# A decoder layer's token mixer: one offset step moved, one pair of VectorE steps swapped, one output tile stored in halves

## The chip, the cores and the metric

The kernel runs on one core of one Trainium2 chip. The core has five engines with queues of their own: TensorE (matrix products), VectorE and ScalarE (elementwise work, and the only ones here that read what TensorE leaves in PSUM), GpSimd, and SyncE, which here issues most of the DMA transfers. The metric is the device time of one execution in microseconds, as the median of several executions.

## The reference

One decoder layer for 512 tokens of width 1024, in float32: a gated feed-forward network, a token mixer, a second feed-forward network, a gated per-token embedding and a final normalisation. The mixer computes `h = h + concat(ya, yb) @ w_out`, with all of its inputs from one projection of the normalised `h`:

```
u, v, z, xbc, dt_raw = split(n @ w_in)
ya = gelu(u) * (tril(w_s) @ layernorm(gelu(v)) + b_s)      # 8 heads of 128, chunks of 128 tokens
ya = rmsnorm(ya)
yb = ssd(silu(conv(xbc)), softplus(dt_raw)) * silu(z)      # 16 heads of 64, chunks of 128 tokens
yb = grouped_rmsnorm(yb)
```

The layernorm of `v` has a gain and a shift for each feature. The shift passes through the product with `tril(w_s)` as (row sum of `tril(w_s)`) x shift, so that for each head an offset "row sum x shift + b_s" can be worked out apart from the data. The SSD part needs for each head a 128 x 128 matrix of decays for each chunk, multiplied by C x B.

## The kernel before

Everything is kept feature by token: a tile has 128 features on the partitions and 512 tokens along the row. Each float32 product is made of three passes over operands split in a high and a low part, so each weight block is cast on ScalarE (`cast`, line 537, gives `whi`) and its remainder taken on VectorE (`low`, line 541, gives `wlo`).

The work is a list of steps, and each step has a product on TensorE and pieces of work for the other engines. The function `run` writes out a fixed order: in the body of step n come the product of step n, then the cast of step n+2 (ScalarE), the pieces called "after" of step n-1, the remainder `low` of step n+2 (VectorE), the pieces called "post" of step n-1, and last the pieces called "rest" of step n, which are TensorE's. The four engines TensorE, ScalarE, VectorE and SyncE keep the order in which the code issues their instructions; only data and buffers make one wait for another. In the mixer `first(n, f)` puts f among the "after" pieces of body n, `post(n, f)` among its "post" pieces, `on_pe(n, f)` among its "rest" pieces. Within one list, pieces stand in the order in which the code registers them.

The mixer's steps are listed in `ORDER`. Those that matter here are numbers 29 to 34: u0, z6, u1, z7, u2, u3. A z step projects one tile of z, which is then opened (`gate_begins`: times the token factor on VectorE, line 1663, tanh on ScalarE, line 1666) and closed (`gate_ends`, line 1670). Pair j of SSD heads goes with z tile j: its rows are loaded, `decayed` forms the decays on ScalarE (lines 1619 and 1623), `times_cb` masks both of them with C x B on VectorE (line 1627), `ssd` runs the pair's products on TensorE (lines 1637 and 1644), and `gated` takes them up in the next step (lines 1654 and 1655 on VectorE, 1656 and 1657 on GpSimd).

The gating heads go in two sets of four, `spatial(n, q)` with q = 0 at n = 29 and q = 1 at n = 31. In body n the weights and biases are loaded, in n+1 GpSimd masks them, in n+2 they are split (line 192 on ScalarE, line 193 on VectorE) and TensorE sums their rows (`sums`, line 1737, in a PSUM bank of its own), and in n+3 `offsets` (line 1741, four instructions of VectorE) multiplies the sums by the shift and adds the bias. So in body 31 TensorE sums the first set, in body 32 VectorE forms the first offsets, in body 33 TensorE sums the second set, and in body 34 the second offsets are formed. Head i's product with the normalised `v` is `mixed(i)` (line 1819), the first in body 33 behind the second sums; `mix_kept` (line 1826) takes it up in body 34 with the offsets. The normalisation of `v` itself ends with `v_factor` (line 1777 and the lines of `rsqrt`, 240 to 246) in body 32 and eight instructions `v_normed` (line 1782) in body 33.

So body 33 holds, on TensorE: the product of u2, `ssd(7)`, the second sums, `mixed(0)`. On VectorE: the opening of z7, the masking of pair 7, the remainder of the second spatial weights, the eight `v_normed`, `low` of step 35, the closing of z7.

PSUM banks are handed out by helpers. Tiles with the same tag share the buffers of that tag in turn, and a new tile in a buffer waits until the last reader of the old one is done. The ring for z tiles, SSD, sums and mixed heads takes three banks "sm" and every fourth time the single bank "a1":

```
def ring_ps():
    turns["ring"] += 1
    return bank("a1", 1) if turns["ring"] % 4 == 0 else sm_ps()
```

The u products use three banks "mm" and one "a0" instead. Between the two spatial sums the ring is used by z7 and twice by `ssd(7)`.

At the end of the kernel the output is turned back to tokens by features (`turn`), scaled and stored (`row_out`) in eight tiles of 128 tokens by 512 features: four of the first half of the tokens, then, behind the last normalisation factor, four of the second half, taken in turn by ScalarE (line 2014) and VectorE (line 2016), each with a DMA on SyncE's queue (line 2017).

## Time and profile before

| | |
|---|---|
| median of 3 runs | 1015.7 us (1015.55 to 1015.75) |
| the profiled execution's own time | 1015.54 us |
| its span, first to last instruction | 1013.8 us |
| TensorE busy | 1004.2 us (99%) |
| VectorE busy | 844.8 us (83%) |
| ScalarE busy | 581.1 us (57%) |
| GpSimd busy | 134.5 us (13%) |
| DMA | 168.89 MB, 167 GB/s on average |

The profile shows one execution. In it PE is TensorE's matrix products, PEld its weight loads, DVE VectorE, ACT ScalarE, POOL GpSimd, SP SyncE, and a q behind a name the queue that issues. A row of a timeline is: start in us from the span's start, duration in us, engine, line of the kernel, operation, output <- inputs by the program's names without their numbers, shapes, and how many instructions are merged in it; what stands in brackets is the idle time ahead of it and who ended it. A row of the chain of waits is: start, duration, engine, tile and line. Neighbouring instructions of one engine overlap by some tenths of a microsecond in their records, so the step from one start to the next is a better measure of what one costs than its duration.

### The profile page before, as it was taken

How to read it: one execution, taken by the hardware profiler on the slowest of the kernel's cores; microseconds unless marked ns; L12 is line 12 of the kernel's file. 1: busy time of each engine (PE TensorE's matmuls, PEld its weight loads, DVE VectorE, ACT ScalarE, POOL GpSimd, SP SyncE). 2: the span in 40 equal slices, each digit the busy share in tenths (PEclk: the TensorE clock that was granted, in tenths of full speed). 3: DMA queues.
4: the chain of work that ended last, by engine and by line, in shares of the span. 5: the costliest groups of instructions: out<-in, count | busy, mean ns of one | idle time of the engine just before them, and what ended most of it. 6: DMA issues, size and time to landing. Idle time of an engine off the chain costs nothing.

```text
span 1013.8 us, 18324 instructions
## 1 busy us (share of the span) xinstructions
PE 1004.2 (99%) x7464; PEld 948.9 (94%) x7464; DVE 844.8 (83%) x1114; ACT 581.1 (57%) x780; POOL 134.5 (13%) x141
## 2 busy tenths in 40 slices
PE   9999999999999999999999999999999999999997
PEld 7899999999999899888888888899999999999987
DVE  7988888879988897876999757778888888988886
ACT  7755545456667474675754434455545446665765
POOL 0101001002311000044333000101010000330101
PEclk9999999999999999999999999999999999999999
DMA  9977678649972333544432324837777655995412
GB/s 340 335 210 200 186 208 199 197 146 226 206 172 64 95 116 96 161 150 125 134 117 84 104 104 141 218 114 186 196 208 201 175 167 208 215 211 138 166 63 84
DMA packets 51188, 168.89 MB, mean 167 GB/s; under 512 B 5792, under 2 KB 6304, under 8 KB 51104
## 3 DMA queue, kind: packets, MB, share of 16 engines
q1 hardware_dynamic: 39440, 125.71, 36.5%
q0 software_dynamic: 11520, 41.95, 22.3%
q8 instruction: 58, 0.95, 0.4%
q14 instruction: 26, 0.21, 0.1%
q10 hardware_dynamic: 144, 0.07, 0.0%
HBM read 163.44 MB, written 4.26 MB: 165 GB/s over the span
## 4 chain that ended last, share of the span: by engine, by line
PE 89%; DVE 7%; ACT 1%; issue 1%; DMA 1%; SPq 0%; DVEq 0%; ACTq 0%
PE mm L753 21%; PE a L753 15%; PE a L1139 8%; PE mm L231 6%; PE sm L217 6%; PE mm L1139 5%; PE sm L1139 5%; PE mm L217 5%; PE sm L231 4%; PE a L217 4%; PE a L231 3%; DVE wlo L541 2%; PE sm L847 2%; PE a L847 1%; PE mm L847 1%
## 5 line engine op out<-in xcount | busy, mean ns | idle before, releaser
L541 DVE TENSOR_TENSOR wlo<-raw,whi 128x1024 fp32r<-128x1024 f32 (+2 forms) x162 | 199.5, 1232 | 57.9 <-ACT whi L537 57.8
L537 ACT CAST whi<-raw 128x1024 fp32r<-128x1024 f32 (+2 forms) x162 | 166.5, 1033 | 134.7 <-DVE raw L763 31.0
L753 PE MATMUL mm<-xfb,whi 128*128 128x256 f32 x960 | 163.8, 275 | 0.0
L753 PEld LDWEIGHTS mm<-xfb,whi 128*128 128x128 f32 x960 | 145.7, 192 | 0.0
L753 PE MATMUL mm<-xfb,wlo 128*128 128x256 f32 x480 | 132.0, 275 | 0.0
L537 ACT CAST whi<-rawb 128x1024 fp32r<-128x1024 f32 x76 | 79.8, 1050 | 62.8 <-DVE rawb L763 29.4
L541 DVE TENSOR_TENSOR wlo<-rawb,whi 128x1024 fp32r<-128x1024 f32 x76 | 92.9, 1222 | 21.2 <-ACT whi L537 20.5
L753 PE MATMUL a<-xfb,whi 128*128 128x256 f32 x640 | 109.4, 275 | 0.0
L753 PEld LDWEIGHTS a<-xfb,whi 128*128 128x128 f32 x640 | 97.1, 192 | 0.0
L753 PEld LDWEIGHTS mm<-xfb,wlo 128*128 128x128 f32 x480 | 92.2, 192 | 0.0
L753 PE MATMUL a<-xfb,wlo 128*128 128x256 f32 x320 | 88.1, 275 | 0.0
L1139 PE MATMUL a<-xfb,whi 128*128 128x256 f32 x480 | 80.7, 275 | 0.0
L1139 PEld LDWEIGHTS a<-xfb,whi 128*128 128x128 f32 x480 | 72.9, 192 | 0.0
L768 POOL DMA_DIRECT2D raw<-in_ffn_gu x20 | 17.3, 864 | 398.8 <-DVE G L915 120.2
L217 PE MATMUL sm<-x,whi 128*128 128x512 f32 x224 | 68.3, 387 | 0.0
L1139 PE MATMUL a<-xfb,wlo 128*128 128x256 f32 x240 | 66.0, 275 | 0.0
L911 ACT ACTIVATE G<-G 128x512 f32<-128x512 f32 x40 | 25.4, 634 | 66.4 <-DVE G L909 65.3
L753 PEld LDWEIGHTS a<-xfb,wlo 128*128 128x128 f32 x320 | 61.4, 192 | 0.1
L753 PE MATMUL a<-xfa,whi 128*128 128x256 f32 x320 | 54.7, 275 | 0.1
L753 PE MATMUL mm<-xfa,whi 128*128 128x256 f32 x320 | 54.8, 275 | 0.0
L1139 PE MATMUL mm<-xfb,whi 128*128 128x256 f32 x320 | 53.8, 275 | 0.0
L1139 PE MATMUL sm<-xfb,whi 128*128 128x256 f32 x320 | 53.8, 275 | 0.0
(428 smaller groups left out, 2607.0 us busy)
## 6 DMA issues: line engine op xcount, KB each, us to landing
raw<-in_ffn_gu SPq DMA_DIRECT2D x56, 512.0 KB, 5.0
rawb<-in_ffn_gu SPq DMA_DIRECT2D x32, 512.0 KB, 8.4
raw<-in_w_in SPq DMA_DIRECT2D x28, 512.0 KB, 3.6
s<-in_ffn_gu SPq DMA_DIRECT2D x20, 512.0 KB, 5.7
raw<-in_ffn_gu POOLq DMA_DIRECT2D x20, 512.0 KB, 6.0
s<-in_ffn_gu POOLq DMA_DIRECT2D x20, 512.0 KB, 9.6
rawb<-in_ffn_dw POOLq DMA_DIRECT2D x18, 512.0 KB, 8.1
raw<-in_w_out SPq DMA_DIRECT2D x16, 512.0 KB, 3.3
```

The lines of the kernel that those rows point to most:

```text
L217: nc.tensor.matmul(ps, w, turned(x), start=first and n == 0, stop=last and n == 2, skip_group_check=True)
L231: nc.tensor.matmul(ps[:, tok], wt[:, c], turned(xt[:, tok]), start=first and k == i == 0, stop=last and k == len(xs) - 1 and i == len(by_p ...
L537: nc.scalar.copy(self.hi[:, c], self.raw[:, c])
L541: nc.vector.tensor_tensor(self.lo[:, c], self.raw[:, c], self.hi[:, c].bitcast(F32), ALU.subtract)
L753: nc.tensor.matmul(o, wt[:, c], turned(xt), start=fresh and p == m == n == 0, stop=last and n == 2, skip_group_check=True,)
L768: nc.gpsimd.dma_start(w21.raw, self.src[0], accum_op=ALU.add)
L847: nc.tensor.matmul(ps, (whi, whi, wlo)[n][:, c], t[:, 0:2, n % 2].rearrange("p s (b i) -> p s i b", b=2), start=not lower and p == n == 0, ...
L911: nc.scalar.activation(t, t, AF.Silu)
L1139: nc.tensor.matmul(o, wt[:, c], xt, start=i in (1, 7) and t == jj == n == d % 2 == 0, stop=t == nt - 1 and jj == 1 and d % 2 == 1 and n == ...
```

## The change

There are three edits. First, for the last of the eight pairs only, the masking of the decays (`times_cb(7)`) is issued ahead of the opening of z7 (`gate_begins(7)`) instead of behind it. Second, the offsets of the first set of heads are formed in body 33 instead of body 32, in the list of "post" pieces behind the closing of z7; those of the second set stay in body 34. Third, the first of the last four output tiles, ScalarE's `row_out(2, 0)`, is scaled in two halves of 256 features, each with a DMA of its own.

```diff
-        first(n + 1, lambda j=j: (gate_begins(j), times_cb(j)))
+        first(n + 1, lambda j=j: (times_cb(j), gate_begins(j)) if j == ND - 1 else (gate_begins(j), times_cb(j)))
...
-        post(n + 3, offsets)
+        post(n + 4 - q, offsets)
...
-    def row_out(c, q, on_act):
+    def row_out(c, q, on_act, parts=whole):
         ps, rt = ple["rows", c, q], ple["rt", halves[c // 2].start]
         o = sb("o")
-        if on_act:
-            nc.scalar.activation(o, ps, AF.Copy, scale=rt[:, c % 2 : c % 2 + 1])
-        else:
-            nc.vector.tensor_scalar(o, ps, rt[:, c % 2 : c % 2 + 1], None, ALU.mult)
-        nc.sync.dma_start(out[c * P : (c + 1) * P, q * T : (q + 1) * T], o)
+        for f in parts:
+            if on_act:
+                nc.scalar.activation(o[:, f], ps[:, f], AF.Copy, scale=rt[:, c % 2 : c % 2 + 1])
+            else:
+                nc.vector.tensor_scalar(o[:, f], ps[:, f], rt[:, c % 2 : c % 2 + 1], None, ALU.mult)
+            nc.sync.dma_start(out[c * P : (c + 1) * P, q * T + f.start : q * T + f.stop], o[:, f])
...
-        row_out(2, 0, True)
+        row_out(2, 0, True, halves)
```

## The prediction

> **What bounds the kernel now.** I read the page first, then what TensorE waited for, then the chain of waits around the first two edits and the end of the timeline for the third.

> ```profile
> span 1013.8 us, 18324 instructions
> PE 1004.2 (99%) x7464; PEld 948.9 (94%) x7464; DVE 844.8 (83%) x1114; ACT 581.1 (57%) x780; POOL 134.5 (13%) x141
> ```
> ```profile
> PE sm L174 <- DVE tmp L171: 1.7, 1, 1.7
> PE sm L847 <- DVE wlo L541: 0.6, 1, 0.6
> PE sm L1993 <- DVE sq L1972: 0.5, 1, 0.5
> ```

> TensorE is busy 1004.2 of 1013.8 us, and the three waits listed (the start, the opening of the second FFN, the end) come to 2.8 us. So nothing in the middle can give back more than fractions of a microsecond, while any stall put into TensorE's queue there goes into the end almost whole: behind the edits the only idle left to absorb it is that 0.6 us, which the edit's stall does not touch, because VectorE and TensorE both move later by it. Around the edits the chain of waits reads:

> ```profile
> 520.57 1.21 DVE u L1627 x2
> 521.78 0.04 issue
> 521.82 0.98 PE sm L1637 x13
> ...
> 522.91 0.66 PE sm L1644 x11
> 523.56 0.66 PE a L1737 x2
> ```

> Here VectorE masks the two decays of pair 7 (L1627), and only then TensorE runs that pair's products (L1637, L1644). Behind them stand the spatial sums of the second heads (L1737, the second such pair in the kernel). The timelines of TensorE, VectorE and ScalarE give the same place with its backlog:

> ```profile
> 510.09 0.73 PE L1737 MATMUL a<-convin,onesr 128*128 128x512 f32 x2
> ...
> 520.80 0.38 PE L217 MATMUL mm<-x,wlo 128*128 128x512 f32 x1
> ```
> ```profile
> 515.13 1.11 DVE L1741 SCALAR_TENSOR_TENSOR xs<-a,vec,xs 128x128 f32<-128x128 f32 x4
> 516.16 0.42 DVE L1777 BATCH_NORM_AGGREGATE vstat<-bnst 128x2 f32<-128x12 f32 x4
> ...
> 519.88 0.68 DVE L1663 SCALAR_TENSOR_TENSOR tmp<-sm,rall 128x512 f32<-128x512 f32 x1
> 520.48 1.28 DVE L1627 TENSOR_TENSOR u<-u,ya 128x512 f32<-128x512 f32 x2
> 521.77 0.69 DVE L193 TENSOR_TENSOR convin<-xs,convin 128x512 fp32r<-128x512 f32 x1
> 522.38 3.74 DVE L1782 TENSOR_SCALAR ya<-ya,vstat,vr 128x512 f32<-128x512 f32 x8
> 526.03 1.23 DVE L541 TENSOR_TENSOR wlo<-raw,whi 128x1024 fp32r<-128x1024 f32 x1
> 527.16 0.69 DVE L1670 SCALAR_TENSOR_TENSOR tmp<-tmp,tmp 128x512 f32<-128x512 f32 x1
> 527.76 0.75 DVE L1654 SCALAR_TENSOR_TENSOR xs<-xs,vec,sm 128x512 f32<-128x512 f32 x1
> ```
> ```profile
> 520.60 0.63 ACT L1666 ACTIVATE tmp<-tmp 128x512 f32<-128x512 f32 x1 [3.19 <-DVE tmp L1663]
> 521.14 0.60 ACT L192 CAST convin<-xs 128x512 fp32r<-128x512 f32 x1
> ```

> Two things matter. VectorE is about a step behind TensorE: the L1670 at 527.16, the closing of z tile 7, still belongs to the step whose product TensorE ended at 521.18. And both spatial sums, at 510.09 and 523.56, are written to a tile called "a": of the banks that their helper hands out (three "sm", one "a1") only "a1" prints so. It exists once.

> **Edit 1, masked decays ahead of the opening.** It adds and removes nothing. L1627 needs decays of ScalarE, which stand ahead of tanh there; ScalarE had been idle for 3.19 us before its tanh at 520.60, so they were ready by 517.41 and the masking can go first; it then ends earlier by the pitch of the opening, 520.48 - 519.88 = 0.60 us. TensorE, free at about 521.18, waits until 521.82 now; 0.64 us is all that the edit, alone or with the next, can gain. What is delayed by 0.6 us is the opening and, behind it, tanh and the cast of the second spatial weights on ScalarE.

> **Edit 2, the first heads' offsets a step later.** The four L1741 at 515.13 leave VectorE's queue, which makes all behind them earlier by 516.16 - 515.13 = 1.03 us. I take all of it: one operation in that stretch was slowed beside work of GpSimd, and meets the same work. So the decays start at 519.88 - 1.03 = 518.85, the opening at 518.85 + 1.29 = 520.14 and ends about 520.75. Tanh follows at 520.77, the cast 0.54 behind it (521.14 - 520.60) at 521.31, ending at 521.91. L193 needs that cast and starts at 521.93 instead of 521.77: VectorE loses the gain again by idling. TensorE, meanwhile, starts the pair's products at 521.18 and ends them about 522.85.

> Now comes what the edit puts in. The offsets read the first heads' spatial sums out of "a1". The ring of banks is taken in the order: first sums, z tile 7, the two of pair 7, second sums. That is four turns on, so the second sums need the very bank that the offsets must first have read. Before, the offsets were done at 516.24 and the second sums at 523.56 never waited. After, the offsets stand at the end of VectorE's step, behind L193, the eight L1782, the weight split L541 and the closing of z tile 7 (L1670). Those take 527.76 - 521.77 = 5.99 us from L193's start, so the offsets start at 521.93 + 5.99 = 527.92 and end 1.11 later, at 529.03. TensorE takes its work in order: behind the waiting sums are queued the first mixed head and the whole next product, so nothing fills the gap. The sums start about 529.05 instead of 523.56: **5.5 us later**, with 529.05 - 522.85 = 6.2 us of idle TensorE before them (the 0.64 us of edit 1 is inside this and gains nothing). Both bounds of this term come from the same rows: if VectorE does not idle before L193 it is 5.3, if it is slowed by another 0.3 it is 5.8.

> Nobody else is late by more. VectorE's next step (gated pair 7, first mixed tile) starts 1.3 us later than now and then waits for TensorE, so its backlog shrinks. No queue is passed but VectorE's: the offsets issue no DMA.

> **The clock behind a 6.2 us gap.** No gap of that length stands in the trace between its first and last matmul, but its two ends show what the clock does around one.

> ```profile
> 1006.64 1.04 PE L2008 MATMUL mm<-ident,h 128*128 128x128 f32 x8
> ```
> ```profile
> 1010.80:1011.20 0.40, 0.00 (x0) 0.00 (x0) 0.00 (x0) 0.00 (x0) 0.00 (x0) 0.99 0.98 364
> 1011.20:1011.60 0.40, 0.00 (x0) 0.00 (x0) 0.00 (x0) 0.00 (x0) 0.00 (x0) 0.50 0.74 277
> ```
> ```profile
> 1.66 3.36 PE L174 MATMUL sm<-tmp 128*128 128x512 f32 x7 [1.66 <-DVE tmp L171]
> ...
> 8.07 0.81 PE L1231 MATMUL sm<-ghi,wlo 128*128 128x512 f32 x3
> 8.72 0.38 PE L1231 MATMUL a<-ghi,wlo 128*128 128x512 f32 x1
> ```

> The last matmul ends at 1007.68 and the granted clock (the column of 0.99 and 0.50) falls to half at 1011.2, 3.5 us later. At the start seven matmuls take 3.36 us, 0.48 each, and from 8.07 on three take 8.72 - 8.07 = 0.65, 0.22 each: TensorE ran slow for up to 8.07 - 1.66 = 6.4 us from its first matmul. A gap of 6.2 us is longer than 3.5, so the work after it starts at half clock, and every slow microsecond costs half of one. Bounds: nothing (the clock holds) and 3.2 us (slow for 6.4). I take a slow stretch of 4.8 us, between the 3.5 that the fall took and the 6.4 of the start, nearer the middle because some of the start's matmuls also waited for inputs: **2.4 us**.

> [...]

> **Edit 3, one of the last tiles in halves.** The four last stores now:

> ```profile
> 1007.18 0.69 ACT L2014 ACTIVATE o<-a,rlast 128x512 f32<-128x512 f32 x1 [0.30 <-PE mm L2008]
> ```
> ```profile
> 1003.18 0.51 ACT L1958 ACTIVATE tmp<-tmp,vec 128x256 f32<-128x256 f32 x1 [0.28 <-DVE tmp L1957]
> ```
> ```profile
> 1007.90 0.33 SPq L2017 DMA_DIRECT2D out<-o  x1
> ...
> 1009.29 0.41 SPq L2017 DMA_DIRECT2D out<-o  x1
> ```
> ```profile
> 1010.00:1011.00 1.00, 0.00 (x0) 0.00 (x0) 0.00 (x0) 0.00 (x0) 0.00 (x0) 1.00 1.02 379
> ```

> A half tile costs ScalarE about 0.51 us instead of 0.69, so the first half is stored 0.18 us sooner (issue at 1007.72), and there are five issues where there were four. Four issues span 1009.29 - 1007.90 = 1.39 us, 0.46 from one to the next; five span 1.85, and the last starts at 1007.72 + 1.85 = 1009.57, 0.28 later than now. ScalarE's second tile ends about 0.3 later, which the issues hide. But from 1010 to 1011 the DMA engines are full (share 1.02), and there the end goes by when the bytes start: up to 0.18 earlier. So between -0.18 and +0.28; I take 0, as the two limits meet within a few tenths.

> **The sum.** 5.5 + 2.4 + 0 = 7.9 us on the profiled run's own 1015.54 (span 1013.8, 1.74 outside it), that is 1023.4; on the median of 1015.7, **1023.6 us**.

> **The rivals.** *The clock holds through the gap.* Same stall, no slow stretch: 1015.7 + 5.5 = 1021.2. For it: the 3.5 us of the end was seen once, and could depend on when the gap begins. Against it: the gap is 1.8 times as long. Decides at a fall time over 6.2 us. Chance 0.18. [...]

> *The bank is not waited for* (the other side, not slower). If the second sums landed in any other bank than the one the offsets read, one turn of the ring more or less between them, TensorE would run through: the pair's products start at 521.18, not 521.82, gaining 0.6, and the offsets finish at 529, ahead of the first mixed tile that needs them. 1015.7 - 0.6 = 1015.1, within what can be told from no change. For it: the profile leaves bank numbers out. Against it: both L1737 rows print "a", and the edit adds no turn. Chance 0.10.

> *The end is held by the issuing queue*: +0.3 on top of any case; it changes no sign.

> **How the numbers follow.** The forecast (stall and slow clock) has 0.69, its own range 1022.4 to 1025.0 (5.3 + 1.7 to 5.8 + 3.2 + 0.3). The clock holding 0.18, at 1020.8 to 1021.8. No wait 0.10. 0.03 is left for what I do not see. A range of 1020.7 to 1025.0 leaves out the no-wait case and the tails. A measurement of this kernel can tell about 0.2%, 2 us, from no change: slower takes the first two cases and most of the rest (0.88), same the no-wait case (0.11), and no case gives a gain of 2 us (0.01).

> **What would show it.** In the changed profile: a wait of TensorE on L1741 of about 6 us at 523, L1737 near 529.0 behind the offsets at 527.9 to 529.0; L1627 at 518.9 with L1663 behind it; a granted clock of 0.5 somewhere in 526 to 534, and matmuls of L217 about 0.43 us apart there; five stores at the end, the last issued 0.2 to 0.3 later relative to the last matmul. It is wrong if L1737 stands right behind L1644, if the offsets run before the L1782, or if the clock column stays at 1.0 through the gap.

## The result and the profile after

The changed kernel takes 1024.76 us (1023.32 to 1024.9, five runs) where the kernel before takes 1015.7. The ratio is 1.0081, with a 95% interval of 1.0070 to 1.0091, that is 8.2 us slower by the ratio (7.1 to 9.2) and 9.1 between the medians. The profiled execution took 1024.59 us, with a span of 1022.9, so 9.05 us more than the one before (1015.54).

The first place to look is what TensorE waited for, in the changed kernel:

```profile
PE a L1737 <- DVE xs L1741: 7.2, 1, 7.2
PE sm L174 <- DVE tmp L171: 1.7, 1, 1.7
PE sm L847 <- DVE wlo L541: 0.7, 1, 0.7
```

One wait is new, and it is the one the prediction named: the second spatial sums on the first offsets, 7.2 us. TensorE's timeline there shows its two ends, and slow products behind it:

```profile
522.41 0.82 PE L1644 MATMUL sm<-ya,yb 128*64 128x128 f32 x12
530.40 1.19 PE L1737 MATMUL a<-convin,onesr 128*128 128x512 f32 x2 [7.17 <-DVE xs L1741]
531.39 1.91 PE L1819 MATMUL sm<-xs,ya 128*128 128x128 f32 x8
```

VectorE's timeline shows why the offsets come when they do:

```profile
515.95 0.80 DVE L240 TENSOR_SCALAR nv<-vstat 128x4 f32<-128x4 f32 x1
516.78 0.56 DVE L241 TENSOR_SCALAR ny<-nv 128x4 int32<-128x4 int32 x1
...
517.96 1.19 DVE L243 TENSOR_TENSOR nt<-ny 128x4 f32<-128x4 f32 x1
...
520.05 1.28 DVE L1627 TENSOR_TENSOR u<-u,ya 128x512 f32<-128x512 f32 x2
521.25 0.68 DVE L1663 SCALAR_TENSOR_TENSOR tmp<-sm,rall 128x512 f32<-128x512 f32 x1
523.14 0.69 DVE L193 TENSOR_TENSOR convin<-xs,convin 128x512 fp32r<-128x512 f32 x1 [1.21 <-ACT convin L192]
523.75 3.73 DVE L1782 TENSOR_SCALAR ya<-ya,vstat,vr 128x512 f32<-128x512 f32 x8
...
529.14 1.12 DVE L1741 SCALAR_TENSOR_TENSOR xs<-a,vec,xs 128x128 f32<-128x128 f32 x4
```

The masking (L1627) now stands ahead of the opening (L1663), L193 waits 1.21 us for its cast, and the offsets follow the whole step. The granted clock is the third column from the right. In two stretches of 1 us, and one of 9 us between them, it reads:

```profile
526.00:527.00 1.00, 0.00 (x0) 0.00 (x0) 1.00 (x4) 0.51 (x1) 0.00 (x0) 0.57 0.00 0
527.00:536.00 9.00, 5.60 (x17) 4.88 (x18) 6.98 (x14) 0.63 (x1) 2.27 (x2) 0.50 0.20 60
536.00:537.00 1.00, 1.00 (x5) 0.83 (x4) 1.00 (x5) 0.00 (x0) 0.00 (x0) 0.81 0.19 33
```

A mean of 0.57 in the first means that the clock fell at 526.14; 0.81 in the last, that it rose at 536.38. The products from 530.40 to 536.38 ran at half speed: L217 takes 0.43 us from one product to the next there, and 0.22 behind it.

Each execution starts a little differently: this one is 0.38 us late ahead of all three edits (L1655 of pair 6 at 512.87 instead of 512.49). Where places in the middle of two traces are compared below, each trace's own start, read at this row, is taken off.

### The profile page after: what moved, and what is told of

It reads as the page before. It is cut to its first block, busy times and chain, and to the rows that moved or that the text cites. A ratio compares the mean times of both kernels' runs of the same rounds, so it can differ in the third digit from the quotient of the medians.

```text
span 1022.9 us, 18326 instructions
## 1 busy us (share of the span) xinstructions
PE 1006.7 (98%) x7464; PEld 950.9 (93%) x7464; DVE 843.2 (82%) x1114; ACT 581.0 (57%) x781; POOL 132.7 (13%) x141
## 5 line engine op out<-in xcount | busy, mean ns | idle before, releaser
L541 DVE TENSOR_TENSOR wlo<-raw,whi 128x1024 fp32r<-128x1024 f32 (+2 forms) x162 | 199.4, 1231 | 57.9 <-ACT whi L537 57.7
L541 DVE TENSOR_TENSOR wlo<-rawb,whi 128x1024 fp32r<-128x1024 f32 x76 | 92.7, 1219 | 21.3 <-ACT whi L537 20.5
L217 PE MATMUL sm<-x,whi 128*128 128x512 f32 x224 | 68.3, 387 | 0.0
```

The lines of the kernel that those rows point to most:

```text
L217: nc.tensor.matmul(ps, w, turned(x), start=first and n == 0, stop=last and n == 2, skip_group_check=True)
L541: nc.vector.tensor_tensor(self.lo[:, c], self.raw[:, c], self.hi[:, c].bitcast(F32), ALU.subtract)
```

## The experiments

Ratios are to runs of the kernel before on the same chip. Microseconds given beside a ratio are the ratio less one, times 1016.

**Offsets alone.** The kernel before with `post(n + 4 - q, offsets)`.

> Edit 2 alone: the first heads' offsets in body 33, everything else as before. Theory (the second spatial sums wait for the bank that the first offsets still have to read, and the clock falls in that gap): TensorE waits for L1741 as in the changed kernel, but the opening of z7 is not behind the masking here, so L193 need not idle 1.2 us for its cast, and the wait is about 1.2 us shorter, some 6 us; the clock still falls. Time 1015.7 + 5.3 + 2.4 = about 1023.4, at least 1021. Rival (the swapped opening, with the cast behind it, is what holds TensorE): within 0.5 us of 1015.7.

Measured: 1.0066 (1.0052 to 1.0079), 6.7 us slower. The wait and the clock are there without the swap and without the halves; VectorE's rows show L193 right behind the masking, with no idle time.

```profile
PE a L1737 <- DVE xs L1741: 5.5, 1, 5.5
```
```profile
522.19 0.69 DVE L193 TENSOR_TENSOR convin<-xs,convin 128x512 fp32r<-128x512 f32 x1
528.19 1.12 DVE L1741 SCALAR_TENSOR_TENSOR xs<-a,vec,xs 128x128 f32<-128x128 f32 x4
```

The clock column of two stretches gives its fall at 527.94 and its rise at 534.78:

```profile
527.00:528.00 1.00, 0.00 (x0) 0.00 (x0) 1.00 (x2) 0.00 (x0) 0.00 (x0) 0.97 0.00 0
534.00:535.00 1.00, 1.00 (x5) 0.79 (x4) 1.00 (x2) 0.46 (x1) 0.00 (x0) 0.61 0.00 0
```

So edit 2 carries most of the loss.

**Swap alone.** The kernel before with `(times_cb(j), gate_begins(j))` for the last pair.

> Edit 1 alone: pair 7's masked decays ahead of the opening of z7. Theory: no wait for the bank, the clock column stays at 1.0, time within 0.6 us of 1015.7. By the prediction's term it would be 0.6 us faster. Worked out anew from the changed kernel's trace, the opening delayed by 1.2 us delays tanh, the cast and L193 by as much, and with L193 the second sums and the first mixed head: 0.3 to 0.5 us slower. Rival (the swap holds TensorE): 1021 or more.

Measured: 1.0014 (1.0005 to 1.0022), 1.4 us slower, and not 0.6 faster. The clock holds. The waits are short, and one is new, for GpSimd's sum of squares:

```profile
PE sm L307 <- POOL ssum L281: 0.3, 1, 0.3
PE a L1737 <- DVE convin L193: 0.2, 1, 0.2
```

TensorE's first mixed head shows the rest of it. It is stretched, to 1.77 us from 1.05 before, because its four parts come as the first four L1782 do, and those stand behind L193, which waited for its cast:

```profile
522.76 0.69 DVE L193 TENSOR_TENSOR convin<-xs,convin 128x512 fp32r<-128x512 f32 x1 [1.20 <-ACT convin L192]
```
```profile
524.06 1.77 PE L1819 MATMUL sm<-xs,ya 128*128 128x128 f32 x8
```

So the opening is the start of a chain through ScalarE (tanh, then the cast in the same queue) back to VectorE. Delaying it by 1.2 us costs more than the earlier masking gives.

**Halves alone.** The kernel before with `row_out(2, 0, True, halves)`.

> Edit 3 alone: the first of the last four tiles in halves. By the two traces, from the last normalisation factor to the end the changed kernel took 6.19 us and the one before 6.60. If that 0.4 us is the edit's, 1015.3; if it is chance of the tail, 1015.7 with the last store issued 0.3 us later. No theory has it above 1016.1.

Measured: 1.0001 (0.9992 to 1.0009). These times can't tell 0.4 us from nothing: their interval reaches from 0.8 faster to 0.9 slower. The traces say a little more. From the end of the last product to the end of the span pass 5.7 us in each of the seven traces that have the halves with other edits and 5.9 here, but 5.9 to 6.8 in the four without them (6.1 in the kernel before). So the halves seem to shorten the tail by some tenths of a microsecond.

**Another bank, first attempt.** All three edits, and

```diff
-            got["ps"] = ring_ps()
+            got["ps"] = bank("mm", 3) if q else ring_ps()
```

> All three edits, but the second spatial sums take a bank of the u products' three instead of the ring's turn, so that they need not wait for the first offsets; VectorE's order is that of the changed kernel. Theory (the bank): the 7 us wait and the slow clock go altogether, and TensorE waits only for L193 and the first v_normed, under 1.5 us; time 1015 to 1016.5. Rival (VectorE's backlog or the delayed cast, not the bank): the wait stays on another line, 1021 or more.

Measured: 1.0070 (1.0057 to 1.0083). By the expectation's letter the rival won. The wait's row tells otherwise:

```profile
PE a L1819 <- DVE xs L1741: 6.0, 1, 6.0
```

The sums did not take their turn of the ring, so the first mixed head became the fourth user after the first sums, got "a", and waited in their place. The edit had moved the collision instead of removing it. It does show that the wait belongs to the bank, whoever asks for it.

**Another bank, with the turn used up.** As the last, but `turns["ring"] += 1` when q is 1.

> All three edits; the second spatial sums use up their turn of the ring but are written to one of the three banks of the u products, so that the first mixed head keeps its bank too and nobody takes the bank of the first sums before the fifth turn. VectorE's order is that of the changed kernel. Theory (whoever takes the fourth turn waits for the bank until the offsets have read it): no wait above 1 us at 523, no fall of the clock; what remains is the delayed opening, so the time is that of the swap alone, about 1.0 to 1.4 us above the kernel before. Rival (VectorE's lateness as such): TensorE still loses 5 us or more, on another line.

Measured: 1.0027 (1.0015 to 1.0038), 2.7 us slower. VectorE's order is that of the changed kernel, yet the long wait is gone, and no other of its size has come:

```profile
PE sm L307 <- POOL ssum L281: 1.3, 1, 1.3
...
PE mm L1739 <- DVE convin L193: 0.2, 1, 0.2
```

This settles the bank. It also shows two costs that the expectation missed (1.0 to 1.4 was given, and no fall of the clock). First, the late offsets delay the gating of pair 7, GpSimd's sum of squares follows later, and TensorE waits 1.3 us for it where the swap alone has 0.3. Second, the clock did fall in the profiled execution, 15 us later than in the changed kernel, just behind the products that had waited:

```profile
539.73 1.05 PE L307 MATMUL sm<-ones,ssum 128*128 128x1 f32 x8 [1.32 <-POOL ssum L281]
```
```profile
541.00:542.00 1.00, 1.00 (x10) 1.00 (x9) 0.95 (x2) 1.00 (x2) 0.97 (x1) 0.77 0.19 74
544.00:545.00 1.00, 1.00 (x4) 0.82 (x3) 0.83 (x6) 0.00 (x0) 0.00 (x0) 0.53 0.00 0
```

By the means of 0.77 and 0.53 it was low from 541.54 to 544.94. Product by product, TensorE's lateness against the kernel before grows by 0.7 us up to the mixed heads (the delayed opening), by 1.3 in the wait for GpSimd, and by 1.7 over the low stretch. So of what this execution lost, nearly half is the clock's.

**Offsets ahead of the normalised v.** All three edits, with `first(n + 4, offsets) if q == 0 else post(n + 3, offsets)`.

> All three edits, but in body 33 the first offsets stand behind the opening of z7 and ahead of L193 and the eight v_normed, in the 1.2 us that VectorE idles there in the changed kernel. Theory: the bank is read by about 523, as the second sums come; no wait above 1 us, no fall of the clock; 0.8 to 1.4 us above the kernel before, as the swap alone. Rival (the bank is never in time once the offsets leave body 32): 5 us or more above.

Measured: 1.0003 (0.9994 to 1.0012): no wait for the bank is left, with the offsets still in body 33 and the same bank. It is their place behind 6 us of VectorE's work that made the bank late. The time is below the 0.8 to 1.4 us expected; in the trace TensorE does lose 1.0 us up to L307, much as with the swap alone (1.2), and the tail behind the last product is 0.5 us shorter than before.

**The gap filled.** All three edits, and ahead of the second sums

```diff
+            if q:
+                fill = bank("mm", 3)
+                for _ in range(28):
+                    nc.tensor.matmul(fill, ones_r, x[0][0], start=True, stop=True)
             got["ps"] = ring_ps()
```

> All three edits, and 28 products of 128x512 that nothing reads, some 6.0 us of work, put between pair 7's products and the second sums, where the changed kernel's TensorE waited 7.2 us. Theory (a stall of 6.4 us, and 2.9 us more because the clock falls behind it): the clock column stays at 1.0, the sums start where they did, and the time is 2.9 us below the changed kernel's: about 6.1 us above the kernel before. Rival (the 2.9 us beyond the stall are lost elsewhere, in later waits for VectorE): the time stays at 9 us above.

Measured: 1.0052 (1.0039 to 1.0065), 5.3 us slower: 2.9 less than the changed kernel's 8.2 by ratio, though the intervals (5.3 +- 1.3, 8.2 +- 1.1) lie close. The sums still wait for the offsets, and the clock column is 1.00 on both sides:

```profile
524.40 6.80 PE L1738 MATMUL mm<-x,onesr 128*128 128x512 f32 x28
531.63 0.71 PE L1741 MATMUL a<-convin,onesr 128*128 128x512 f32 x2 [0.43 <-DVE xs L1745]
```

The traces give the difference more sharply. The next mixed heads start, before, in the changed kernel and here, at:

```profile
530.13 1.95 PE L1819 MATMUL sm<-xs,ya 128*128 128x128 f32 x16
```
```profile
539.90 1.95 PE L1819 MATMUL sm<-xs,ya 128*128 128x128 f32 x16
```
```profile
538.24 1.95 PE L1823 MATMUL sm<-xs,ya 128*128 128x128 f32 x16
```

This profiled execution was 1.60 us late from its start (L1655 of pair 6 at 514.09), the changed kernel's 0.38. So the changed kernel had lost 539.90 - 530.13 - 0.38 = 9.39 us by then and this one 538.24 - 530.13 - 1.60 = 6.51. Added work made the kernel faster, and 2.9 us of the loss are the clock's.

**The gap half filled.** The same with 12 products.

> As the filled gap, but with 12 such products, 2.6 us, so that some 4.6 us of idle TensorE are left. If the clock falls a fixed 3.5 us after the last product, it falls in every execution and the time is near 9 us above the kernel before. If it falls at the end of a whole idle window of 3.4 us that runs on its own (the changed kernel's low stretch lasted 10.2 us, three times 3.41), it falls in about (4.6 - 3.4)/3.4, one execution in three, and the times form two groups, near 6 and near 8.5 us above.

Measured: 1.0074 (1.0060 to 1.0087); single runs at 1023.07, 1023.62, 1023.76, 1023.98 and 1025.49. There are no two groups, so neither rule was right as it was put. The profiled execution:

```profile
523.54 3.06 PE L1738 MATMUL mm<-x,onesr 128*128 128x512 f32 x12
530.80 0.71 PE L1741 MATMUL a<-convin,onesr 128*128 128x512 f32 x2 [4.19 <-DVE xs L1745]
```
```profile
531.00:532.00 1.00, 1.00 (x7) 0.91 (x7) 0.77 (x2) 0.00 (x0) 0.15 (x1) 0.81 0.86 344
535.00:536.00 1.00, 1.00 (x6) 0.89 (x5) 1.00 (x3) 0.12 (x1) 0.00 (x0) 0.99 0.00 0
```

The clock fell at 531.62, 0.8 us after TensorE had gone back to work and 5.0 after the last filling product; in the changed kernel it fell 2.9 after the last product. That is not a fixed delay. It rose at 535.02.

**The swap with an early cast.** The swap alone, with the cast of the second spatial weights in body 32.

> Edit 1 alone, with the cast of the second spatial weights moved ahead on ScalarE, into body 32, where ScalarE idled 3 us before; offsets and last tiles as before. Theory (the swap alone is slower because the delayed opening delays tanh, the cast behind it, L193 and the eight v_normed, for which the first mixed head waits): VectorE no longer idles 1.2 us ahead of L193, pair 7's products start 0.5 us earlier and the first mixed head is not later than before; between 0.6 us faster and equal to the kernel before. Rival (the swap costs through something else, the late opening itself): still 1.0 to 1.4 us slower.

Measured: 1.0008 (0.9999 to 1.0017): inconclusive, and no better than the kernel before. The trace says more than the time. L193's idle time is gone, and with it what the swap alone loses: L307 starts 0.05 us earlier than before (537.65 - 537.29 - 0.41 of a late start), where with the swap alone it starts 1.2 later. The execution lost its time behind the last product, in a tail of 6.8 us instead of 6.1, which this edit doesn't touch. Nor did the swap gain anything even so: the early cast pushed back the square behind it on ScalarE (L280), and with it GpSimd's addition (L281), both by 1.65 us; the addition, from 519.55 on, now ran beside the masking, which took 2.37 us for 1.28:

```profile
519.25 2.37 DVE L1627 TENSOR_TENSOR u<-u,ya 128x512 f32<-128x512 f32 x2
```

**GpSimd's work left out.** All three edits, with `if j != 6:` ahead of the two GpSimd operations of `gated`.

> All three edits, but the two GpSimd operations that gate pair 6 (1656 and 1657) are left out, so that this pair's y lacks its state part and its gate. The changed kernel's v_factor stretch took 4.55 us on VectorE where 3.7 stood before, with the offsets ahead of it. Theory (what the offsets gave up was taken again by small operations that now run beside GpSimd): lines 240 and 241 shrink from 0.80 and 0.56 to about 0.35 and 0.2, the stretch to about 3.7, and the remainder L541 ahead of it from 1.64 to 1.2; the second sums come 1.2 us earlier. Rival (these small operations are slow of themselves there): the stretch stays at 4.5.

Measured, in a single execution of 1021.5 us:

```profile
513.78 1.21 DVE L541 TENSOR_TENSOR wlo<-raw,whi 128x1024 fp32r<-128x1024 f32 x1
514.91 0.41 DVE L1778 BATCH_NORM_AGGREGATE vstat<-bnst 128x2 f32<-128x12 f32 x4
515.36 0.17 DVE L240 TENSOR_SCALAR nv<-vstat 128x4 f32<-128x4 f32 x1
515.56 0.17 DVE L241 TENSOR_SCALAR ny<-nv 128x4 int32<-128x4 int32 x1
...
517.42 2.37 DVE L1627 TENSOR_TENSOR u<-u,ya 128x512 f32<-128x512 f32 x2
```

Lines 240 and 241 shrink to 0.17 each, from 0.80 and 0.56 in the changed kernel, and L541 to 1.21 from 1.64: they had been slowed by GpSimd's work. The stretch from L1778 to the masking is 517.42 - 514.91 = 2.51, shorter than the 3.7 expected, because GpSimd's addition (L281) met the masking instead, which took 2.37 for 1.28. The second sums came 1.4 us earlier (1.2 expected).

## Why the prediction was right, and where it was off

*The wait for the bank* was right in mechanism and place: shown by the wait's own row, by the offsets alone, and by the run with another bank. Its size was 530.40 - 523.56 - 0.38 = 6.46 us where 5.5 was forecast. The mis-sized term is "I take all of it", the 1.03 us by which VectorE was to be earlier once the offsets left its queue. The masking started at 520.05, only 519.88 + 0.38 - 520.05 = 0.21 earlier. The forecast held that the operations behind "meet the same work" of GpSimd. They met more: the offsets take 1.11 us beside GpSimd and 1.12 without it, so they had been filling a stretch in which they were not slowed, and when they left, lines 240 and 241 moved into it and took 0.80 and 0.56 where they had taken 0.35 and 0.17 before. That is 0.84 more, and the run without GpSimd's work, with 0.17 each, shows that it is GpSimd's doing. The remaining 0.1 is the step from the offsets' end to the sums, 0.14 instead of 0.02.

Not every operation was slowed beside GpSimd's work: the offsets were not, lines 240 and 241 were, L541 took 1.64 for 1.21, and L1627 takes 2.37 instead of 1.28 in two runs. What sets them apart, no run here separates.

*The clock* fell as forecast. The slow stretch was 536.38 - 530.40 = 5.98 us instead of 4.8 and cost 2.99 instead of 2.4, because the clock stayed low for 10.24 us, from 526.14 on, which the 4.8, the author's estimate from between 3.5 and 6.4, did not foresee; the filled gap shows 2.9 of it.

*The halves* were taken at 0, between -0.18 and +0.28. In the changed kernel's tail the last of the nine stores is issued at 1019.1:

```profile
L2018 SPq DMA_DIRECT2D out<-o x9: 332/379/404, 1013.5 to 1019.1; - x9
```

Counted from the last factor's first use (1007.20 before, 1016.71 after) that is 2.4 us where it was 2.1, about the 0.28 forecast. The end nevertheless came 0.46 sooner after that use (the use is 9.51 later, the end 9.05), so later issuing did not set the end. The traces with the halves all have a shorter tail, so this term was probably mis-sized: a gain of 0.46 lies outside its range. Why it is more than the 0.18 by which the first half is stored sooner stays open.

*The sum* of the profiled run: 0.38 late at its start, 6.46 of wait, 2.99 of slow clock, 0.30 regained at L307, for whose sum of squares TensorE waited before and did not after the stall, and 0.46 regained in the tail. That is 0.38 + 6.46 + 2.99 - 0.30 - 0.46 = 9.07, against 9.05 measured and 7.9 forecast. The wait and the clock together cost 1.5 us more than forecast. The two small gains, less the late start, hid 0.4 of that; the forecast had none of the three, so this part of its closeness is luck.

*The swap* was costed wrongly as an edit by itself: "0.64 us is all that the edit, alone or with the next, can gain" left the delayed opening without a price, although the next sentence named the chain behind it. Alone it loses 1.4 us, and the trace with the early cast, in which this loss is gone, bears the chain out. Inside the change its loss is the 1.21 us that L193 idles, which the forecast counted.

*The rivals.* That the bank is not waited for is refuted. That the clock holds did not happen in any of the five profiled executions with 4 us or more of idle TensorE (4.2 to 7.2), and once it fell behind a wait of 1.3; that it could hold in another execution cannot be excluded. No version beat the kernel before.

## What to carry to other kernels

An operation that reads PSUM also frees a bank, so before moving it later in a queue, count the turns of its ring to the next user and see which engine stands there; where, as on TensorE here, the work is in a fixed order and without slack, nearly the whole wait becomes time (6.46 us here), and the clock may add to it (2.99 here). When testing such a collision, keep the turn and change only the bank, or the next in line inherits the wait. And the operation taken out of a queue may have been the one that its stretch suited best: what moves into its place need not run at its old speed (here lines 240 and 241, at 0.80 and 0.56 us for 0.35 and 0.17).

## What the runs showed that was not expected

The 3.41 us ahead of a fall need not be wholly idle. With the gap half filled, those that ended at 531.62 held 0.8 us of products, from 530.80 on. With another bank and the turn used up, those from 538.13 to 541.54 held one idle stretch of 1.3 us, and behind it 0.9 us of products one column wide (L307) and 0.9 us of mixed heads: in this execution the clock fell behind a short wait beside small products. How much each of the two counts, no run here separates. Nor did 3.41 us that were mostly busy raise the clock: in the changed kernel the middle third of the low stretch, 529.55 to 532.97, held 2.6 us of work at half clock, and the clock rose only 3.41 us later.
